# A mixture-of-experts stage on one core: slots and gather of a block three blocks ahead instead of two, and another order of units

## Chip, cores and metric

The kernel runs on one core of a Trainium2 chip. The metric is the device time of one execution in microseconds (us), the median of several runs.

## What is computed

One decoder block on 512 tokens of width 1024: a mixer (a Mamba-2 state-space branch and a short convolution), then a mixture of experts. The change touches the experts alone. Of the reference, cut:

```python
e_idx = top_k(where(expert_mask, biased, -inf), 8)[1]        # 8 of 64 experts for each token
gate = take_along_axis(scores, e_idx, axis=1); gate = gate / gate.sum(-1) * 2.5
...
xin = h_pad[row_tok].reshape(nb, 128, d)                     # tokens sorted by expert, in blocks
def expert_block(xb, e):                                     # D_EXPERT = 256
    return (silu(xb @ w_gate[e]) * (xb @ w_up[e])) @ w_down[e]
routed = segment_sum(yb * row_gate[:, None], row_tok)        # back to the tokens
x = layer_norm(ALPHA * x + g2 * (routed + shared)) * ln2_g + ln2_b
```

All is float32. The weights of the 64 experts are 3 MB each and are read once.

## The kernel before

The first 860 us (norms, projections, state-space scan, output projection, router) are not touched. The expert stage follows. Experts are ranked by their number of tokens, and each rank has a fixed number of slots (`CAPS`: 320, 192, 160, 128, 96, 64, 32). Slots are packed into **blocks** of 128: a block belongs to one expert (then matmuls run in three passes on split weights, `matmul3`, lines 153 to 155) or to two to four experts side by side in the columns of the array (`tiled`, line 950, plain fp32).

Blocks are grouped into **units** by the string `ORDER`, one word a unit, one letter a group of ranks: `x` and `y` and `z` are the large ranks with their remainders (x three blocks, y and z two), `f` a full block, `a` a 96+32 pair, `p` two times 64, `q` four times 32. So ya, za, qy, qff and faa have three blocks, ap has two; qy and qff load six experts, ya, za and ap four, faa five. The first unit (two ranks with a fixed place, one block) is ordered by the framework's scheduler; from the second on PE's order is the program's own (`manual_schedule`), while DVE, ACT, POOL and SP are ordered by the scheduler.

For each block `slots` (lines 1108 to 1135) makes, for its 128 slots, which token sits there: DVE compares positions with a counter (`oh`, line 1116), PE multiplies the one-hot with the tokens' numbers and gates (line 1124, into the one `st` bank), DVE reduces that to `red` (1127) and to the index `idx` (1129), and POOL issues an indirect DMA that gathers the 128 rows of `h2_d` into a page (line 1132; in the profile `pg<-h_d,idx`). There are `NXG` = 3 such pages, used in turn. `xsteps` (from line 897) then transposes the page in two times four PE transposes (line 150, `ps_tr<-ident,pg`, two `tr` banks), and ACT (line 911 or 158), for a block of one expert also DVE (line 160), copies the bank into `xt`.

A unit (`unit`, from line 1410) runs: gate and up matmuls of its blocks (`ps_pj`), then a mixed stretch, here called the **hand-over**: PE adds the unit before's results to the tokens (`csteps`, lines 1188 and 1189, eight steps, one part a block), with the transposes of its own activations (`ps_tr<-ident,sg`) and then those of the next unit's blocks (`xs_steps`) in between; then its down matmuls (`ps_y` of lines 153 to 155 and 950). In `xs_steps` the slots are made like this:

```python
while len(xs) < min(n, len(allb)):
    i = len(xs)
    need_s(i + 1)
    r, g = xsteps(sl[i][0], None, len(allb[i][0]) > 1)
    xs.append(r)
    yield from g
    need_s(i + NXG)
```

So after block i is transposed, blocks up to i+2 have their slots and gathers. Weights come on SP's queue (lines 869 and 872) in pieces of 1 MB, each expert's gate and up in two halves and its down, into seven pairs of pages and, for every eighth piece, one from a second pool; a piece waits until the matmuls have freed its buffer. Weights of single-expert blocks are split by ACT (line 158, `wh<-pr`) and DVE (160, `wl<-pr`).

Of the kernel before, what the change touches and what calls it, by code (L numbers as in the profile page):

```python
# [8 lines left out]
F32 = mybir.dt.float32  # L9
# [9 lines left out]
T, D, P = 512, 1024, 128  # L19
# [18 lines left out]
NXG = 3  # L38


ORDER = "x qy ya ap za qff ya ap za faa ya ap za faa p"
AHEAD = 10
NDEF = 2
FORD = "q0 r0 s0 q1 r1 s1 q2 r2 s2 q3 r3 s3"
# [19 lines left out]
def block_kernel(ctx: ExitStack, tc: tile.TileContext, a, out, dbg=None):  # L64
# [25 lines left out]
    def bank(tag, bufs, dt=F32):  # L90
        return ps.tile([P, 512], dt, name="ps_" + tag, tag=tag, bufs=bufs)
# [645 lines left out]
    rt = ctx.enter_context(tc.tile_pool(name="rt", bufs=1))  # L737
# [159 lines left out]
    def xsteps(src_ap, dst=None, whole=False):  # L897

        hi, lo = dst or [None if whole and i else hold.tile([P, KD, P], F32 if whole else FR, name="xt", tag="hm", bufs=8)
                         for i in range(2)]  # L900
        sv = src_ap.rearrange("p (d k) -> p k d", k=KD)

        def steps():
            for q in range(2):
                tp = bank("tr", 2)
                for k in range(4):
                    transpose(tp[:, k * P:(k + 1) * P], sv[:, 4 * q + k, :])
                tv = tp.rearrange("p (k n) -> p k n", k=4)
                sl_ = slice(4 * q, 4 * q + 4)
                if whole:  # L910
                    S.activation(hi[:, sl_, :], tv, AF.Copy)
                else:
                    split_to(hi[:, sl_, :], lo[:, sl_, :], tv)
                yield

        return (hi, lo), steps()
# [191 lines left out]
    def slots(*parts):  # L1108


        oh = rt.tile([P, NT, P], BF, name="oh", bufs=2)
        w = min(n for _, n, _ in parts)
        i, tiles = 0, []
        for v, n, pays in parts:
            m = len(pays)
            V.tensor_tensor(oh[:, :, i:i + n * m].rearrange("p t (q s) -> p t q s", q=m),
                            iota1[:, None, None, :n].to_broadcast([P, NT, m, n]),
                            v[:, :, :, None].to_broadcast([P, NT, m, n]), op=OP.is_equal)
            i += n * m
            tiles += [p_ for p_ in pays for _ in range(n // w)]  # L1120
        ip = bank("st", 1)
        for t in range(NT):
            for q, p_ in enumerate(tiles):
                PE.matmul(ip[w * q:w * q + w, :6], oh[:, t, w * q:w * q + w], p_[:, t],
                          start=(t == 0), stop=(t == NT - 1), tile_position=(0, w * q) if w < P else None)
        red = rt.tile([P, 2], F32, name="red", bufs=8)
        V.tensor_reduce(red, ip[:, :6].rearrange("p (a b) -> p a b", b=3), axis=AX.X, op=OP.add)
        idx = rt.tile([P, 1], I32, name="idx", bufs=4)
        V.tensor_scalar(idx, red[:, 0:1], NOTOK, None, op0=OP.add)
        xg = xgs[nblk[0] % NXG]  # L1130
        nblk[0] += 1
        GP.indirect_dma_start(out=xg, out_offset=None, in_=h2_d[:, :],  # L1132
                              in_offset=bass.IndirectOffsetOnAxis(ap=idx, axis=0),
                              bounds_check=T - 1, oob_is_err=False)
        return xg, red
# [101 lines left out]
    def static_slots(u):  # L1237
        return slots((pg[:, :, 0, u[0]:u[-1] + 1], P // len(u), [pays[:, :, e, :] for e in u]))
# [61 lines left out]
    def seg(r, n, m=1, v=None):  # L1300
        return (posp if v is None else v)[:, :, r:r + m], n, [pay[:, :, r + i, :] for i in range(m)]

    def second(r):
        pc = rt.tile([P, NT, 1], F32, name="pc")
        V.tensor_scalar(pc, posp[:, :, r:r + 1], 128.0, None, op0=OP.subtract)
        return slots((pc, P, [pay[:, :, r, :]]))
# [6 lines left out]
    for r in range(NM):  # L1313
        bl = [((0,), lambda r=r: slots(seg(r, P)))]
        if r == 0:
            bl.append(((0,), lambda r=r: second(r)))
        n = caps[r] % 128
        r2 = of[128 - n].pop(0)
        bl.append(((0, 1) if n == 64 else (0, 1, 1, 1),
                   lambda r=r, n=n, r2=r2: slots(seg(r, n, 1, posr), seg(r2, 128 - n))))  # L1320
        kinds["x" if r == 0 else "y" if n == 64 else "z"].append(((r, r2), bl))
# [5 lines left out]
    for k, n in (("p", 64), ("q", 32)):  # L1327
        m = 128 // n
        for r in of[n][::m]:
            kinds[k].append((tuple(range(r, r + m)),  # L1330
                             [(tuple(range(m)), lambda r=r, n=n, m=m: slots(seg(r, n, m)))]))
    for ks in ORDER.split():

# [18 lines left out]
    def need_s(n):  # L1352
        while len(sl) < min(n, len(allb)):
            sl.append(allb[len(sl)][1]())

    def xs_steps(n):
# [3 lines that stand above are left out]
            r, g = xsteps(sl[i][0], None, len(allb[i][0]) > 1)  # L1360
            xs.append(r)
            yield from g
            need_s(i + NXG)

    def need_x(n):
        drain(xs_steps(n))
# [43 lines left out]
    def unit(n):  # L1410


        i0, i1 = ublk[n], ublk[n] + len(units[n][1])
        i2 = i1 + len(units[n + 1][1]) if n + 1 < len(units) else i1
        need_x(i1)
        run = expert([b for b, _ in units[n][1]], units[n][2], sl[i0:i1], xs[i0:i1], lambda e, q: take((n, e, q), AHEAD))
        for _ in range(2 * len(units[n][2])):
            next(run)
        com = csteps() if parts else iter(())
        for _ in range(2):  # L1420
            next(com, None)
        for _ in range(i1 - i0):
            next(run)
            next(com, None)
        zipper(xs_steps(i2), com, islice(over_, 1))
        next(run)
        tail[0] = n + 1 == len(units)
        drain(run)
# [113 lines left out]
```

## Time and profile before

| | us |
|---|---|
| runs | 1625.51, 1630.03, 1628.57 |
| median | 1628.57 |
| the profiled execution, its own time | 1629.32 |
| its span, first to last instruction | 1627.5 |
| PE busy in the span | 1496.8 (92%) |
| mean granted clock of TensorE | 0.972 of full speed |
| expert stage, about | 860 to 1605 |

The page gives busy time by engine, then the span in 40 slices of 40.7 us each. "Granted clock" is TensorE's clock as a share of full speed. A row of the timeline has start, length, engine, line, operation, tiles written and read, shapes and count; in brackets the idle time of that engine ahead of it and what ended it. A row of waits has who waited, for whom, us in total, times, longest.

### The profile page before, as it was taken

The page shows a single profiled execution, that of the slowest core. Times are in us where ns is not written, and L with a number is a line of the kernel's source. Part 1 is how long each engine was busy: PE and PEld are TensorE (multiplying, and loading weights), DVE is VectorE, ACT ScalarE, POOL GpSimd, SP SyncE. Part 2 cuts the span into 40 slices and gives each one's busy share as a digit, 9 for nine tenths or more (in the row PEclk, how much of TensorE's full clock was granted, in tenths as well). Part 3 has the DMA queues.
Part 4 walks back from the last instruction along what each step waited for, and adds up shares of the span by engine and source line. Part 5 has one row for each costly group of instructions (what it writes and reads, how often), then busy time and mean ns, then how long its engine had stood idle before and what let it go on. Part 6 is the DMA issues. An engine that isn't in the chain of part 4 may idle for free.

```text
span 1627.5 us, 22863 instructions
## 1 busy us (share of the span) xinstructions
PE 1496.8 (92%) x8253; PEld 1018.3 (63%) x8253; DVE 974.6 (60%) x1810; ACT 645.4 (40%) x925; POOL 230.3 (14%) x232
## 2 busy tenths in 40 slices
PE   6999999999999999999978899988889988998893
PEld 3688777787777877887755544545544555554452
DVE  4558778667858556536786535545554554444456
ACT  2456575655634545334542213222341232222222
POOL 0011110111012457300135000000010000000001
PEclk9999999999999999999999999999999999999997
DMA  9653432533441667536227677877988878877671
GB/s 277 170 154 88 113 70 83 147 85 97 117 100 39 203 202 217 167 91 212 108 77 289 234 283 286 305 297 302 386 303 304 309 255 358 317 301 297 253 302 53
DMA packets 194504, 335.67 MB, mean 206 GB/s; under 512 B 13428, under 2 KB 136660, under 8 KB 186196
## 3 DMA queue, kind: packets, MB, share of 16 engines
q1 hardware_dynamic: 183300, 303.73, 53.9%
q0 software_dynamic: 11088, 30.45, 7.3%
q8 instruction: 66, 1.08, 0.3%
q14 instruction: 50, 0.41, 0.1%
HBM read 334.58 MB, written 4.28 MB: 208 GB/s over the span
## 4 chain that ended last, share of the span: by engine, by line
PE 68%; DMA 12%; DVE 8%; issue 6%; ACT 3%; POOL 1%; SPq 1%; DVEq 0%; ACTq 0%; POOLq 0%
PE ps_pj L153 12%; PE ps_pj L154 12%; PE ps_pj L155 12%; PE ps_pj L950 6%; DMA pr<-in_w_up_dram 5%; PE ps_y L950 5%; PE ps_y L1188 4%; PE ps_y L1189 4%; PE ps_tr L150 4%; DMA pg<-h_d,idx 4%; DMA pg<-in_w_ada_dram 2%; DVE wl L160 2%; PE ps_y L153 1%; PE ps_y L155 1%; PE ps_y L154 1%
## 5 line engine op out<-in xcount | busy, mean ns | idle before, releaser
L153 PE MATMUL ps_pj<-hm,wh 128*128 128x512 f32 x680 | 276.3, 407 | 2.0 <-ACT wh L158 2.0
L155 PE MATMUL ps_pj<-hm,wl 128*128 128x512 f32 x680 | 267.4, 394 | 6.2 <-DVE wl L160 6.2
L154 PE MATMUL ps_pj<-hm,wh 128*128 128x512 f32 x680 | 267.4, 393 | 0.0
L160 DVE TENSOR_TENSOR wl<-pg,wh 128x1024 fp32r<-128x1024 f32 (+1 forms) x129 | 157.1, 1224 | 116.9 <-ACT wh L158 116.7
L950 PE MATMUL ps_pj<-pr,xt 128*32 128x512 f32 (+1 forms) x1472 | 212.2, 604 | 9.7 <-DMA pr<-in_w_up_dram 9.7
L158 ACT ACTIVATE wh<-pg 128x1024 fp32r<-128x1024 f32 (+1 forms) x135 | 127.5, 952 | 136.4 <-PE ps_pj L154 104.6
L950 PEld LDWEIGHTS ps_pj<-pr,xt 128*32 128x32 f32 (+1 forms) x1472 | 62.0, 117 | 150.1 <-issue 139.7
L153 PEld LDWEIGHTS ps_pj<-hm,wh 128*128 128x128 f32 x680 | 128.9, 190 | 36.7 <-issue 6.0
L155 PEld LDWEIGHTS ps_pj<-hm,wl 128*128 128x128 f32 x680 | 128.5, 189 | 36.7 <-DVE wl L160 8.8
L154 PEld LDWEIGHTS ps_pj<-hm,wh 128*128 128x128 f32 x680 | 128.5, 189 | 28.9 <-issue 3.4
L160 DVE TENSOR_TENSOR wl<-pr,wh 128x1024 fp32r<-128x1024 f32 x72 | 86.9, 1220 | 96.6 <-ACT wh L158 96.0
L1132 POOL DMA_INDIRECT pg<-h_d,idx x41 | 48.1, 1174 | 597.2 <-PE ps_y L1189 163.6
L1194 DVE TENSOR_TENSOR res<-res,ps_y 128x512 f32<-128x512 f32 x120 | 82.2, 686 | 75.3 <-PE ps_y L1189 73.7
L150 PE MATMUL ps_tr<-ident,pg 128*128 128x128 f32 x392 | 71.1, 314 | 49.0 <-DMA pg<-h_d,idx 45.7
L158 ACT ACTIVATE wh<-pr 128x1024 fp32r<-128x1024 f32 x72 | 74.8, 1054 | 101.5 <-DMA pr<-in_w_up_dram 67.4
L950 PE MATMUL ps_y<-pr,wkr 128*32 128x512 f32 (+1 forms) x736 | 106.1, 618 | 0.8 <-DVE wk L1165 0.8
L150 PEld LDWEIGHTS ps_tr<-ident,pg 128*128 128x128 f32 x392 | 58.9, 196 | 60.5 <-issue 32.6
L1165 DVE SCALAR_TENSOR_TENSOR wk<-ps_y,red,pg 128x512 f32<-128x512 f32 x82 | 61.0, 748 | 35.3 <-PE ps_y L155 20.1
L366 POOL TENSOR_TENSOR pg<-pg 128x1024 f32<-128x1024 f32 x28 | 74.1, 2665 | 54.6 <-ACT pg L364 54.5
L927 ACT ACTIVATE sg<-ps_pj 128x256 f32<-128x256 f32 x44 | 16.8, 384 | 159.7 <-PE ps_pj L950 99.2
L153 PE MATMUL ps_pj<-pg,wh 128*128 128x512 f32 x192 | 76.0, 396 | 1.3 <-ACT zs L431 1.2
L155 PE MATMUL ps_pj<-pg,wl 128*128 128x512 f32 x192 | 76.3, 397 | 0.0
(394 smaller groups left out, 2648.8 us busy)
## 6 DMA issues: line engine op xcount, KB each, us to landing
pr<-in_w_gate_dram SPq DMA_DIRECT2D x128, 512.0 KB, 9.8
pr<-in_w_up_dram SPq DMA_DIRECT2D x128, 512.0 KB, 10.1
pr<-in_w_down_dram SPq DMA_DIRECT2D x64, 1024.0 KB, 11.7
pg<-in_w_in_dram SPq DMA_DIRECT2D x88, 512.0 KB, 4.9
pg<-in_w_ada_dram SPq DMA_DIRECT2D x48, 512.0 KB, 5.9
bc<-acs_d POOLq DMA_DIRECT2D x32, 256.0 KB, 4.5
pg<-in_w_ssd_out_dram SPq DMA_DIRECT2D x16, 512.0 KB, 4.5
pg<-in_w_sc_out_dram SPq DMA_DIRECT2D x8, 512.0 KB, 4.0
```

The costliest lines, as they stand in the source:

```text
L150: return PE.transpose(o, i, ident[:n, :n])
L153: PE.matmul(o, lh, rh, start=start, stop=False)
L154: PE.matmul(o, lh, rl, start=False, stop=False)
L155: PE.matmul(o, ll, rh, start=False, stop=stop)
L158: S.activation(hi, src, AF.Copy)
L160: V.tensor_tensor(lo, src, rw(hi), op=OP.subtract)
L366: GP.tensor_tensor(part[i], part[i], w, op=OP.add)
L950: PE.matmul(o[w * i:w * i + w, :], x[:, w * i:w * i + w], m, start=start, stop=stop, tile_position=(0, w * i))
L1165: V.scalar_tensor_tensor(yg, o, red[:, 1:2], g2b[:, ns_], op0=OP.mult, op1=OP.mult)
L1188: PE.matmul(o, oh_, yh[:, ns_], start=(i == 0), stop=False)
L1189: PE.matmul(o, oh_, yl[:, ns_], start=False, stop=(i == len(ps_) - 1))
L1194: V.tensor_tensor(ra[t][:, ns_], ra[t][:, ns_], o, op=OP.add)
```

## The change

After block i is transposed, slots and gather are made up to block i+3. `red` has ten buffers in place of eight. The same units come in another order: qy third instead of second among the words of `ORDER`, faa twice behind ap instead of behind za.

```diff
-ORDER = "x qy ya ap za qff ya ap za faa ya ap za faa p"
+ORDER = "x ya qy za ap ya qff za ya ap faa za ap faa p"
@@ slots
-        red = rt.tile([P, 2], F32, name="red", bufs=8)
+        red = rt.tile([P, 2], F32, name="red", bufs=10)
@@ xs_steps
-            need_s(i + NXG)
+            need_s(i + 1 + NXG)
```

First place: PE, the hand-over at the end of unit x, in which the next unit's blocks are transposed (`ps_tr<-ident,pg`; x4 is half a block) between steps of the combine (`ps_y<-pr,oht`). Before, from the end of the next unit's first block on; rows of line 1124 are slots (`pay` the tokens' numbers and gates), and of each run of them the first two are shown:

```order
L150 MATMUL ps_tr<-ident,pg 128x128 x4
L1188 MATMUL ps_y<-pr,oht 128x512
L1189 MATMUL ps_y<-pr,oht 128x512
L1124 LDWEIGHTS oh
L1124 MATMUL ps_st<-pay,oh 64x6
...
L150 MATMUL ps_tr<-ident,pg 128x128 x4
L1188 MATMUL ps_y<-pr,oht 128x512
L1189 MATMUL ps_y<-pr,oht 128x512
L150 MATMUL ps_tr<-ident,pg 128x128 x4
L1124 LDWEIGHTS oh
L1124 MATMUL ps_st<-pay,oh 128x6
...
L150 MATMUL ps_tr<-ident,pg 128x128 x8
```

Now, the same stretch:

```order
L150 MATMUL ps_tr<-ident,pg 128x128 x4
L1188 MATMUL ps_y<-pr,oht 128x512
L1189 MATMUL ps_y<-pr,oht 128x512
L1124 LDWEIGHTS oh
L1124 MATMUL ps_st<-pay,oh 32x6
...
L150 MATMUL ps_tr<-ident,pg 128x128 x4
L1188 MATMUL ps_y<-pr,oht 128x512
L1189 MATMUL ps_y<-pr,oht 128x512
L150 MATMUL ps_tr<-ident,pg 128x128 x4
L1124 LDWEIGHTS oh
L1124 MATMUL ps_st<-pay,oh 128x6
...
L150 MATMUL ps_tr<-ident,pg 128x128 x8
```

The pattern is the same; the slots in it are other blocks'. Before, the 64x6 rows make the slots of the very block (qy's third) that the x8 row transposes. Now the 32x6 rows make those of the first block of the unit after (qy's q), and the slots of the block in the x8 row (ya's third) stood ahead of unit x's down and gate matmuls.

Second place: ACT at the hand-over of an ap unit, behind its two `silu` rows (`sg`). `xt` rows empty banks of transposed blocks, `wh<-pr` rows split weights of the coming unit's single-expert block. Before, at all three ap units, and now at the first and third:

```order
L941 ACTIVATE wkr<-ps_tr 128x256 x2
L158 ACTIVATE xt<-ps_tr 128x512 x2
L911 ACTIVATE xt<-ps_tr 128x512
L158 ACTIVATE wh_76<-pr 128x1024
L911 ACTIVATE xt<-ps_tr 128x512
L158 ACTIVATE wh_78<-pr 128x1024
L911 ACTIVATE xt<-ps_tr 128x512 x2
```

Now, at the second ap unit:

```order
L941 ACTIVATE wkr<-ps_tr 128x256 x2
L158 ACTIVATE xt<-ps_tr 128x512 x2
L911 ACTIVATE xt<-ps_tr 128x512 x2
L158 ACTIVATE wh_76<-pr 128x1024
L158 ACTIVATE wh_78<-pr 128x1024
L911 ACTIVATE xt<-ps_tr 128x512 x2
```

There the two splits stand together, ahead of the last block's copies.

Third place: DVE in the first unit. The first `red` and `idx` on either side are those of unit x's third block (the `posr` row belongs to a block of ya); `wl_77` is the lower half of a split weight. One piece of the difference:

```order
-L1160 TENSOR_SCALAR tok<-red 128x1
-L1161 TENSOR_SCALAR oht<-iota_t,tok 128x512
-L160 TENSOR_TENSOR wl_77<-pr,wh_76 128x1024
-L1127 TENSOR_REDUCE red<-ps_st 128x2
-L928 TENSOR_TENSOR sg<-sg,ps_pj 128x256
-L1129 TENSOR_SCALAR idx<-red 128x1
...
+L1127 TENSOR_REDUCE red<-ps_st 128x2
+L1116 TENSOR_TENSOR oh<-iota_5824,posr 128x4x64
+L1129 TENSOR_SCALAR idx<-red 128x1
...
+L160 TENSOR_TENSOR wl_77<-pr,wh_76 128x1024
```

The index is now made ahead of the weight split, not behind it. On PE the slots' matmuls of that block stand nine matmuls (`ps_pj<-pr,xt 64x512`) earlier: before they follow a run of eleven of these, now a run of two. And of unit x's second and third block the transposes now stand, half a block at a time, between the first unit's down matmuls (`ps_y<-pr,wkr 64x512`).

## Rows read from the trace of the kernel before

**Rows 1.** The page, the span in 40 slices: busy tenths of PE and of the DMA engines.

```profile
PE   6999999999999999999978899988889988998893
...
DMA  9653432533441667536227677877988878877671
```

**Rows 2.** PE's waits from 930 to 1600 us: who waited for whom, us in total, times, longest.

```profile
PE ps_tr L150 <- DMA pg<-h_d,idx: 41.8, 10, 5.4
PE ps_pj L950 <- DMA pr<-in_w_up_dram: 9.7, 8, 1.6
PE ps_pj L154 <- DVE wl L160: 4.8, 6, 1.0
```

**Rows 3.** The timeline of all engines in the hand-over from za to qff, 1122 to 1129 us.

```profile
1122.14 0.25 PE L1124 MATMUL ps_st<-pay,oh 128*128 128x6 bf16 x4
...
1123.01 0.40 PE L1189 MATMUL ps_y<-pg,oht 128*128 128x512 f32 x1
...
1123.25 0.40 PE L1188 MATMUL ps_y<-hm,oht 128*128 128x512 f32 x1
1123.35 0.14 DVE L1129 TENSOR_SCALAR idx<-red 128x1 int32<-128x1 f32 x1
...
1123.72 0.61 PE L150 MATMUL ps_tr<-ident,pg 128*128 128x128 f32 x4
...
1124.23 0.99 POOL L1132 DMA_INDIRECT pg<-h_d,idx  x1 [34.86 <-PE ps_y L1189]
1124.36 0.60 ACT L158 ACTIVATE xt<-ps_tr 128x512 fp32r<-128x512 f32 x1 [0.78 <-PE ps_tr L150]
1124.99 0.69 DVE L160 TENSOR_TENSOR xt<-ps_tr,xt 128x512 fp32r<-128x512 f32 x1
...
1128.56 1.94 PE L150 MATMUL ps_tr<-ident,pg 128*128 128x128 f32 x8 [4.16 <-DMA pg<-h_d,idx]
```

**Rows 4.** The chain of work that ended last, in unit x's start: start, us, what.

```profile
888.36 11.16 DMA pg<-h_d,idx
```

**Rows 5.** Seven us from the end of each of the ten waits for a gathered page on: stretch, length, PE busy (matmuls), granted clock, DMA share, GB/s.

```profile
933.80:940.80 7.00, 7.00 (x35) 0.76 0.43 130
991.80:998.80 7.00, 6.96 (x50) 0.76 0.43 126
1084.70:1091.70 7.00, 6.95 (x50) 0.79 0.21 60
1128.60:1135.60 7.00, 7.00 (x44) 0.76 0.23 75
1186.00:1193.00 7.00, 6.96 (x50) 0.76 0.28 74
1279.90:1286.90 7.00, 6.99 (x68) 1.00 0.34 108
1323.90:1330.90 7.00, 6.96 (x31) 0.56 0.30 92
1378.90:1385.90 7.00, 6.96 (x32) 0.59 0.32 96
1471.60:1478.60 7.00, 6.95 (x56) 0.63 0.36 104
1517.90:1524.90 7.00, 7.00 (x36) 0.77 0.03 10
```

**Rows 6.** The same columns for gaps in the weights' stream, from the last landing of one period to SP's next issue, nine of them at hand-overs with such a wait: three of the nine, and the sum of all nine.

```profile
1278.60:1284.60 6.00, 4.68 (x56) 1.00 0.30 99
...
1378.40:1389.20 10.80, 10.26 (x60) 0.71 0.21 63
1471.00:1478.70 7.70, 7.05 (x56) 0.63 0.33 96
...
sum 81.50, PE 69.16; mean PE 7.68
```

**Rows 7.** The same columns for a stream of weights between two gaps, faa behind za.

```profile
1334.50:1378.20 43.70, 38.89 (x290) 1.00 0.97 370
```

**Rows 8.** The timeline of PE at the first unit's start, where two halves of a block are transposed close together.

```profile
876.62 0.71 PE L150 MATMUL ps_tr<-ident,pg 128*128 128x128 f32 x4 [0.69 <-ACT xt L911]
```

**Rows 9.** PE's waits in unit qy's gate and up matmuls (945 to 970 us, the first row) and in qff's (1137 to 1170 us).

```profile
PE ps_pj L950 <- DMA pr<-in_w_up_dram: 3.0, 2, 1.6
...
PE ps_pj L950 <- DMA pr<-in_w_up_dram: 3.2, 2, 1.6
PE ps_pj L154 <- DVE wl L160: 1.5, 2, 0.8
PE ps_pj L153 <- ACT wh L158: 0.5, 1, 0.5
```

**Rows 10.** The timeline of PE in the first unit and at unit x's third block.

```profile
883.51 2.74 PE L950 MATMUL ps_pj<-pr,xt 128*64 128x512 f32 x11
...
899.65 0.95 PE L150 MATMUL ps_tr<-ident,pg 128*128 128x128 f32 x4 [1.90 <-DMA pg<-h_d,idx]
```

**Rows 11.** ACT's waits for weight pieces from 930 to 1600 us, and a split of weights in ACT's timeline at the hand-over of an ap unit.

```profile
ACT wh L158 <- DMA pr<-in_w_up_dram: 64.5, 12, 9.5
...
1077.49 1.05 ACT L158 ACTIVATE wh<-pr 128x1024 fp32r<-128x1024 f32 x1
```

**Rows 12.** The columns of rows 5 for a hand-over whose next unit has two blocks, without a wait.

```profile
1425.00:1432.00 7.00, 7.00 (x50) 1.00 0.40 116
```

## The prediction

> **What bounds the kernel now.** I read the page's slices first, then TensorE's waits in the expert stage, then one hand-over between two units row by row, then the granted clock and the DMA share in short windows. From slice 22 on (the expert stage, about 930 to 1600 us) PE is 80 to 90% and more busy, and the DMA engines 60 to 90% [rows 1]: neither is full, so something stops both. PE's waits name it: 41.8 us in ten waits of the transposes for a gathered page, against 9.7 us for weights and 4.8 us for a split weight [rows 2].
>
> The hand-over shows why [rows 3]. The 1122.14 row makes the slots of the coming unit's third block, after that unit's first block was transposed; its index is ready at 1123.35, POOL issues the gather at 1124.23. PE has one more block to transpose (until about 1124.4), then it stands for 4.16 us, until the page has landed and the 1128.56 row starts. The third block's gather is issued some 4 us before it is needed, with nothing left to cover its landing. Units with two blocks have no such wait: both gathers are a unit old.
>
> The wait has a second price. [...] At a hand-over without a wait the clock stays at 1.00 [rows 12].
>
> **The change, part by part.** (a) *Three ahead.* After block i is transposed, the slots of i+3 instead of i+2 are made. Its page is the one that block i has just left (three pages), so no new wait on POOL for a page arises; PE, POOL and SP issue the same instructions as before, with other blocks' slots at the old places. All blocks of a unit, third one too, now have their gathers issued during the hand-over before: one unit earlier, 44 us between the third and fourth wait [rows 5]. The longest flight in the trace, under full weight traffic, is 11.16 us [rows 4]. So the ten waits go: **-41.8 us** [rows 2].
>
> (b) *The clock they cost.* Per window, lost time is (1 - granted share) x 7 us: 0.24+0.24+0.21+0.24+0.24+0+0.44+0.41+0.37+0.23 = 2.62, times 7 = **-18.3 us** [rows 5]. None of it stays if no other pause follows.
>
> (c) *What is late next on PE.* Two blocks are now transposed back to back at each three-block hand-over, through two banks. The last four transposes need the bank of the four before the previous ones, which ACT empties in 0.60 us, with 0.69 us on DVE behind it for a block of one expert [rows 3]. The nearest row of a transpose waiting for that is 0.69 us [rows 8]. Bounds per hand-over: 0 (the slots' matmuls and four transposes cover it) and 0.60 + 0.69 = 1.3. I take 0.69, since it is that very wait: **+6.9 us** over ten (0 to 13).
>
> (d) *Weights.* SP can load about eight 1 MB pieces ahead (seven pairs and one page pair); it waits for a unit's down matmuls to free them. Order, not work, changes: the same fifteen units. Between the first release of one unit and that of the next it loads the old unit's downs and twice the new unit's experts, less what was preloaded; so qy brings 2+12 = 14 MB now and 4+12 = 16 MB behind ya, as qff does today. PE's weight waits are 3.0 us in qy today and 3.2+1.5+0.5 = 5.2 us in qff [rows 9]: I take the difference, **+2.2 us**. Both faa now follow ap instead of za, so their period is shorter by one part's combine, 16 matmuls 0.24 us apart [rows 3], 3.8 us, for the same 14 MB; today the DMA needs 43.7 us for that [rows 7] and then has a gap of 10.8 [rows 6]. I price this at nothing, covered by that gap; if the cover is gone it costs up to 3.8 us twice. Bounds for (d): 0 and 2.2 + 7.6 = 9.8.
>
> Is the gap large enough for (a) and (b)? SP's releases come after the wait and after the slow stretch, so from one release to the next hand-over nothing moves; what shrinks is the DMA's gap before the next release. The nine gaps at the later waits are 6.0 to 12.4 us long, 81.5 us in all, at shares of 0.11 to 0.46 [rows 6]; the tightest, 1471.0 to 1478.7, is 7.7 us and loses about 4.2 (the mean wait) + 2.6 (its slow stretch) = 6.8. It fits, barely.
>
> (e) *Start.* The third block of unit x waits 1.90 us for a gather that started at 888.36 [rows 4, 10]. The new order makes its slots nine of the x11 matmuls of the 883.51 row earlier, 9/11 of 2.74 = 2.2 us [rows 10], more than the wait: **-1.9 us** (0 to -3.6 with a slow stretch behind it; above zero, +3, if the transposes now placed between the first unit's down matmuls hold those up). (f) `red` from 8 to 10 buffers: nine blocks' results can be alive; no instruction, nothing on the path.
>
> Sum against the profiled execution (1629.3 us; the median of the runs is 1628.6, so within 0.1%): 1629.3 - 41.8 - 18.3 - 1.9 + 6.9 + 2.2 = **1576.4 us**.
>
> **The rivals.** *R1, weights take part of it back.* If the DMA's gaps cannot go under the shortest one seen, 6.0 us, the nine give 81.5 - 9 x 6.0 = 27.5 us, and the first wait, whose gap is wide, 4.2 + 1.7 = 5.9; (c) then hides in the weights' wait. 1629.3 - 33.4 - 1.9 + 2.2 = **1596 us**. For it: a stream between two gaps takes 0.97 of the DMA engines [rows 7], and the gaps hold the next gathers too. Against it: in a gap the share is 0.11 to 0.46 and SP is the one that waits [rows 6].
>
> *R2, the clock is not given back.* The hand-over becomes a run of transposes and short matmuls; if the clock fell there without a wait, (b) would be lost: 1576.4 + 18.3 = **1595 us**. Against it: hand-overs without a wait, transposes included, show 1.00 [rows 12], and the sixth window shows 1.00 although a wait and a block's transposes stand there [rows 5]. [...]
>
> *R3, slower: ACT blocked by a weight copy.* ACT works in order, and at hand-overs copies of coming weights stand between the copies that empty the transposes' banks (the second place shown with the change). Today such a copy at 1077.49 starts without a wait, while ACT's waits for weights, 12 with up to 9.5 us, fall into the gate and up matmuls [rows 11]. If weights fell behind so far that this copy waited 9.5 us at each of ten hand-overs, PE would stand behind it: 1576.4 + 95 = **1671 us**. It turns slower than before once the copy is over 5.3 us late on each (53 / 10). Against it: that needs the DMA stream to be late at every hand-over, and only two or three of the periods have no slack.
>
> *R4, it doesn't do what it says.* If the gather were still issued at the old time (held on POOL behind the page or an index), nothing would change: **1629 us**. Against it: at the new place the page is free and the slots' matmuls stand in PE's order a whole unit before the transposes that need them.
>
> **How the numbers follow.** Forecast with its own bounds 0.65; R1 0.20; R2 0.07; R3 0.05; R4 0.03. The predicted time is 1576 us. Low end 1560: (c) and (d) at zero give 1567.3, (e) at its best 1565.6, and some of today's weight waits (9.7 us) may end with the denser run. High end 1603: the forecast with (c), (d) and (e) at their worst is 1576.4 + 6.1 + 7.6 + 4.9 = 1595, and it takes in R1 and R2 with half of (c) on top. R3 and R4 lie outside, with a few hundredths of the rest. About 0.3% (4.9 us) is what a measurement of this kernel can tell from no change. Faster by more: 0.65 + 0.20 + 0.07 = 0.92; within: 0.03; slower: 0.05.
>
> **What would show it.** Right: PE's waits for the gathered page in the expert stage fall from ten to none, or under 3 us; the granted clock after hand-overs is 1.00; small new waits of the transposes for ACT's or DVE's copies, under 1 us each; the DMA's gaps shrink from 6 to 12 us to 1 to 6; qy waits about 5 us for weights. R1 would show as PE waits for weight pieces of 2 to 4 us in most units; R2 as slow stretches without a pause ahead; R3 as transposes waiting for ACT while ACT waits for a weight; R4 as unchanged gather waits. The forecast is wrong if the ten waits go and the time falls by less than 30 us.

## The result, and the profile after

| | before | changed |
|---|---|---|
| median, us | 1629.30 (1625.51 to 1632.53, 4 runs) | 1583.97 (1580.36 to 1588.03, 4 runs) |
| profiled execution, us | 1629.32 | 1580.36 |
| its span, us | 1627.5 | 1578.6 |
| mean granted clock | 0.972 | 0.983 |

The changed kernel takes 0.972 of the time, with a 95% interval of 0.969 to 0.976: 45 us less. The forecast was 1576 us, in a range of 1560 to 1603. The profiled execution is the fastest of the four.

The page's slices of the changed kernel, PE, the granted clock and the DMA engines, answer to [rows 1]:

```profile
PE   6999989999999999999988999999988999999994
PEclk9999999999999999999999999999999999999997
DMA  9763423632531557634622967998989788997871
```

From slice 23 on PE now shows 8 or 9 tenths in every slice but the last, and the DMA engines 6 to 9. PE's waits from 930 to 1555 us answer to [rows 2] (who waited for whom, us in total, times, longest); eight of the ten largest are:

```profile
PE ps_pj L950 <- DMA pr<-in_w_up_dram: 11.7, 10, 2.3
PE ps_pj L154 <- DVE wl L160: 6.0, 7, 1.7
PE ps_pj L153 <- ACT wh L158: 3.2, 3, 1.4
PE ps_y L154 <- DVE wl L160: 1.6, 1, 1.6
...
PE ps_st L1124 <- DVE oh L1116: 0.8, 1, 0.8
PE ps_tr L150 <- ACT xt L911: 0.8, 1, 0.8
PE ps_tr L150 <- DVE xt L160: 0.6, 1, 0.6
PE ps_st L1124 <- DVE red L1127: 0.4, 1, 0.4
```

The gathered page is no longer among them: 41.8 us in ten waits have become none. The waits for weights and their splits (first four rows) have grown from 14.5 us, and 0.9 for splits by ACT, to 22.5. The hand-over from za to ya in the changed kernel, rows of the timeline of all engines, stands against [rows 3]:

```profile
1253.83 0.60 PE L150 MATMUL ps_tr<-ident,pg 128*128 128x128 f32 x4
...
1254.36 0.29 PE L1124 MATMUL ps_st<-pay,oh 128*64 128x6 bf16 x8
...
1254.59 1.25 PE L150 MATMUL ps_tr<-ident,pg 128*128 128x128 f32 x8
...
...
1256.99 1.12 POOL L1132 DMA_INDIRECT pg<-h_d,idx  x1 [46.96 <-DVE idx L1129]
```

The third block's eight transposes start at once behind the second block's. The gather that POOL issues at 1256.99 is for a block of the unit after ya and has a whole unit to land (the stage's gathers took 3.9 to 9.6 us from issue to landing). The 7 us behind each of the ten three-block hand-overs (columns as in [rows 5]):

```profile
924.20:931.20 7.00, 7.00 (x39) 1.00 0.51 156
970.40:977.40 7.00, 7.00 (x49) 1.00 0.54 168
1022.60:1029.60 7.00, 6.68 (x46) 1.00 0.61 199
1110.10:1117.10 7.00, 6.65 (x50) 1.00 0.45 144
1150.60:1157.60 7.00, 6.17 (x36) 0.76 0.56 187
1206.50:1213.50 7.00, 5.39 (x55) 1.00 0.73 231
1255.80:1262.80 7.00, 6.73 (x53) 1.00 0.40 116
1342.60:1349.60 7.00, 7.00 (x65) 1.00 0.52 166
1386.20:1393.20 7.00, 6.73 (x53) 1.00 0.81 317
1474.60:1481.60 7.00, 7.00 (x48) 1.00 0.30 96
```

Nine of ten are at 1.00, where nine of ten were at 0.56 to 0.79. The tenth stands behind two new pauses, in the hand-over before qff: a transpose waits 0.58 us for DVE's `xt` at 1149.89, the slots 0.83 us for `oh` at 1151.54.

For a sum I take one stretch whose ends are the same work in every kernel: from the end of the wait for `wkr` that opens the expert stage to the end of the last combine's wait for `rww`. First before, then the changed kernel (columns as above):

```profile
862.12:1599.12 737.00, 670.05 (x4204) 0.97 0.79 297
```

```profile
858.64:1549.98 691.34, 658.60 (x4205) 0.99 0.84 316
```

The stage is 45.7 us shorter: PE idles 34.2 us less (67.0 to 32.7) and is busy 11.4 us less. The span fell by 48.9; the remaining 3.2 us lie outside the stage, nearly all ahead of it, where nothing was changed.

### The profile page after: what moved, and what is told of

It reads as the page before. It is cut to its first block, busy times and chain, and to the rows that moved or that the text cites. A ratio compares the mean times of both kernels' runs of the same rounds, so it can differ in the third digit from the quotient of the medians.

```text
span 1578.6 us, 22869 instructions
## 1 busy us (share of the span) xinstructions
PE 1486.1 (94%) x8253; PEld 1010.2 (64%) x8253; DVE 975.3 (62%) x1810; ACT 644.8 (41%) x925; POOL 227.3 (14%) x232
## 4 chain that ended last, share of the span: by engine, by line
PE 73%; DMA 11%; DVE 8%; ACT 3%; issue 2%; POOL 1%; SPq 1%; DVEq 0%; ACTq 0%; POOLq 0%
PE ps_pj L153 12%; PE ps_pj L154 12%; PE ps_pj L155 12%; PE ps_pj L950 8%; DMA pr<-in_w_up_dram 8%; PE ps_y L950 5%; PE ps_y L1188 5%; PE ps_y L1189 5%; PE ps_tr L150 4%; DMA pg<-in_w_ada_dram 2%; DVE wl L160 2%; PE ps_y L153 1%; PE ps_y L155 1%; PE ps_y L154 1%; PE ps_y L483 1%
## 5 line engine op out<-in xcount | busy, mean ns | idle before, releaser
L950 PE MATMUL ps_y<-pr,wkr 128*32 128x512 f32 (+1 forms) x736 | 102.7, 596 | 1.3 <-DVE wk L1165 1.3
L928 DVE TENSOR_TENSOR sg<-sg,ps_pj 128x256 f32<-128x256 f32 x44 | 18.3, 420 | 111.8 <-ACT sg L927 111.8
L153 PE MATMUL ps_pj<-pg,wh 128*128 128x512 f32 x192 | 75.9, 395 | 1.1 <-ACT zs L431 1.1
L154 PE MATMUL ps_pj<-pg,wh 128*128 128x512 f32 x192 | 75.8, 395 | 0.0
L416 DVE SCALAR_TENSOR_TENSOR wk<-ps_pj,cw,wk 128x511 f32<-128x511 f32 (+2 forms) x93 | 68.3, 742 | 7.4 <-ACT wk L414 7.0
```

The lines of the kernel that those rows point to most:

```text
L153: PE.matmul(o, lh, rh, start=start, stop=False)
L154: PE.matmul(o, lh, rl, start=False, stop=False)
L416: V.scalar_tensor_tensor(acc[:, s:], o[:, :T - s], cw[:, 3 - s, tl:tl + 1], acc[:, s:], op0=OP.mult, op1=OP.add)
L950: PE.matmul(o[w * i:w * i + w, :], x[:, w * i:w * i + w], m, start=start, stop=stop, tile_position=(0, w * i))
```

## The experiments

The question that the result left: the prediction's sum, without its term for weights and order, gives 1574 us, and the kernel came out 10 us above. So the two halves of the change were run apart, the price of the clock by itself, and then the order's parts and the weights. Times stand beside runs of the kernel before on the same chip. The stage columns are worked out as above, from each profiled execution; the last column is PE's busy time while the granted clock was at its lower level, 0.50 of full speed (in before's trace from 1129 to 1132 us, in the changed kernel's from 1455.2 to 1458.5, for example).

| run | median, us | ratio to before | stage | PE busy | idle | busy at lower clock |
|---|---|---|---|---|---|---|
| before, profiled as above | 1629.3 | 1 | 737.0 | 670.1 | 67.0 | 46.8 |
| e0 change again | 1584.4 | 0.970 (0.967 to 0.974) | 690.1 | 658.4 | 31.7 | 9.8 |
| e1 three ahead, old order | 1574.0 | 0.965 (0.962 to 0.968) | 677.5 | 651.8 | 25.7 | 0 |
| e2 two ahead, new order | 1639.8 | 1.003 (1.000 to 1.006) | 748.9 | 681.4 | 67.5 | 69.9 |
| e3 the wait filled | 1617.5 | 0.990 (0.986 to 0.994) | 723.4 | 692.8 | 30.6 | 15.6 |
| e4 qy second, faa behind ap | 1580.8 | 0.969 (0.966 to 0.972) | 690.9 | 659.2 | 31.8 | 17.1 |
| e5 qy third, faa behind za | 1576.5 | 0.967 (0.964 to 0.970) | 684.1 | 655.9 | 28.2 | 6.8 |
| e6 change, half of the downs | 1579.5 | 0.967 (0.964 to 0.971) | 686.0 | 659.7 | 26.3 | 13.1 |
| e7 old order, half of the downs | 1577.1 | 0.966 (0.963 to 0.969) | 684.8 | 657.3 | 27.5 | 12.7 |
| e8 change, half of gate and up | 1558.7 | 0.955 (0.952 to 0.958) | 667.9 | 647.1 | 20.8 | 14.4 |
| e9 old order, half of gate and up | 1552.0 | 0.952 (0.949 to 0.955) | 657.2 | 640.6 | 16.7 | 3.4 |

Before's median was 1634.2 us beside e0 to e3, 1631.5 beside e4 to e7 and 1629.9 beside e8 and e9. The stage columns are of one execution each, and not always a typical one: e1's is the second fastest of its eight (1566.4 us) and e9's the fastest, while those of e0, e4, e6 and e8 are the slowest or second slowest of theirs. So stage differences between these are larger than those of the medians.

**The two halves apart: e0, e1, e2.** e0 is the changed kernel again. e1 is the changed kernel with the order of before; e2 is the kernel before with the new order:

```diff
e1, against the change
-ORDER = "x ya qy za ap ya qff za ya ap faa za ap faa p"
+ORDER = "x qy ya ap za qff ya ap za faa ya ap za faa p"
e2, against before: the same line the other way round
```

> The changed kernel once more, so that the three beside it are compared with it under the same conditions. Theory (the gathered page of a third block comes a unit earlier, ten waits and the slow clock behind them go): 1584 us, ratio to before 0.972.

> Three blocks ahead with the old order of units, so the first part alone. Theory (the lead of the gather is the whole gain, the order adds only weight waits): no PE wait for a gathered page left, ratio 0.969 to 0.972, 1579 to 1584 us; the waits for f's split weight in the two faa units, 2.2 + 2.2 us and 1.3 us for a weight in the changed kernel, are back at about 1.2 us each, and qy waits about 3 us for weights in place of 5. Rival (the order is needed for the gain, since units with much to load come in the wrong place once the pauses are gone): over 1595 us, with PE waits for weight pieces above 25 us in all.

> The new order with slots and gather two blocks ahead as before, so the second part alone. Theory (the order alone removes no gather wait, and moves at most some weight waits): ten PE waits for a gathered page, about 42 us, and 1628 to 1635 us, ratio 0.999 to 1.004. Rival (the order has a part in the gain): under 1620 us.

All of the gain comes from three blocks ahead. e1 came out 5 us under the low end of what was expected of it, so the order costs more than was thought then. e1 ran at 1560.8 to 1577.8 us (8 runs), e0 at 1580.1 to 1591.5 (6 runs): the ranges don't touch, and the new order costs 10 us beside it. With two ahead the order gains nothing (e2, 5.6 us above before in the medians, at the edge of what can be told); its ten waits for gathered pages are still there, 39.1 us. e1's stage:

```profile
857.88:1535.35 677.47, 651.77 (x4204) 1.00 0.85 323
```

Against before's 737.0 and 670.05, with the same order: idle time is 41.3 us less and busy time 18.3 us less, and none of the busy time is at the lower clock. That holds for this execution: it and one other have the highest granted clock of e1's eight runs, 0.988; the others have 0.980 to 0.986. The clock is not all that sets e0 and e1 apart: among the runs with 0.980 or 0.981, e0's three took 1580.1 to 1589.8 us and e1's three 1574.3 to 1577.8.

**The price of the clock alone: e3.** The kernel before, with four matmuls on constants ahead of each third block's transposes (`third` holds those blocks), into a bank that is free there:

```diff
+            if i in third:
+                fill = bank("pj", 3)
+                for k in range(NFILL):                        # NFILL = 4
+                    PE.matmul(fill, ident, iota_t, start=(k == 0), stop=(k == NFILL - 1))
```

> The kernel before, with four idle fp32 matmuls of 128x512 (about 3.5 us together, their result is not used) put on PE ahead of the transposes of each third block, where PE waits for the gathered page. The gathers come as late as before, so this shows the price of the clock alone. Theory (each of the ten waits costs 1.5 to 3 us more through the slow clock behind it): the granted clock behind the hand-overs is 1.00, and the time is 1612 to 1618 us, ratio 0.990 to 0.994. Rival (the clock costs little, since what runs behind the wait is not bound by the array's clock): 1625 to 1631 us.

The waits in e3's stage (columns as above), and the fill's own group of instructions (its number and form, then busy us and mean ns):

```profile
PE ps_pj L951 <- DMA pr<-in_w_up_dram: 9.7, 8, 2.2
PE ps_tr L151 <- DMA pg<-h_d,idx: 6.8, 7, 1.9
```

```profile
L1367 PE MATMUL ps_pj<-iota_t,ident 128*128 128x512 f32 x80 | 36.9, 604 | 0.0
```

The 80 records are the 40 matmuls, two each. The third block is no earlier: fill and what is left of the wait make 36.9 + 6.8 = 43.7 us, where the wait alone was 41.8. PE merely works through it, and the kernel is 16.7 us faster in the medians. Without the fill's 36.9 us PE is busy 655.9 us in the stage, 14.1 less than before. So the clock behind a pause is a cost of its own, and near the size that (b) gave it; 15.6 us of e3's work is still at the lower level.

**Which part of the order: e4 and e5.** Both are three ahead. e4 puts qy back to second place and leaves the rest of the new order, e5 moves qy alone:

```diff
e4
+ORDER = "x qy ya za ap ya qff za ya ap faa za ap faa p"
e5
+ORDER = "x ya qy ap za qff ya ap za faa ya ap za faa p"
```

> Three blocks ahead, with qy second as before and the rest of the order as in the change (faa behind ap, qff between ya and za). The full order of the change gave 1584.4 us, the order of before 1574.0. Theory: the price of the order, about 10 us, lies behind qff and in faa behind ap (a shorter period for the same weights), not in qy: 1584 us here, with waits of 1.3 to 1.5 us for up weights in both faa. Rival: qy third is what costs; then this kernel stands at about 1574.

> Three blocks ahead, the order of before with qy moved to third place alone (faa behind za). Theory (faa behind ap and the neighbours of qff cost, qy does not): 1574 us, waits in faa of 0.8 us and no slow clock behind them. Rival (qy third costs): 1584 us, with the waits for weights in qy and ap at 980 to 1050 us larger than the 4 us of the change.

By the ratio e4 stands 0.001 under e0, e5 0.002 above e1, and the intervals of all four overlap their neighbours'. The order of the four is as the theory has it. In the stage e4 has 690.9 us with 31.8 idle, as e0 has, but e5 has 684.1 with 28.2, about halfway between e1 and e0. The rival's sign is there too: e5's waits for weights and a split between 980 and 1060 us are 5.4 us, where the changed kernel's between 980 and 1050 are 3.6. So faa behind ap and qff between ya and za may carry most of the price, but this is not shown: by time e4 and e5 are not told apart.

**Less of the weights: e6 and e7.** Half of each down piece:

```diff
-            SY.dma_start(r, wd.rearrange("(p k) n -> p k n", k=2))
+            SY.dma_start(r[:, 0], wd.rearrange("(p k) n -> p k n", k=2)[:, 0, :])
...
-            return ... else held[e][:, q - 4, :]
+            return ... else held[e][:, 0, :]
```

> The change, but only half of each down piece is loaded (0.5 MB instead of 1 MB; its first half is used twice), so 2.5 MB an expert instead of 3. PE's, ACT's and DVE's work and the order stay. Theory: what is left between the order of the change and that of before is late weights and the slow clock behind them; with a sixth less to load PE's waits for weights (22 us in the change) fall under 8 us, and the time to about 1560 us, within 3 us of the same cut with the order of before. Rival (the order costs on PE, ACT and DVE themselves, by copies that stand in another order at the hand-overs): the waits fall, but this kernel stays some 10 us above the next one.

> Three blocks ahead, the order of before, half of each down piece loaded as in the run before this one. Theory: 1574.0 less about 10 us of its 15 us of waits for weights, so 1562 us, within 3 us of the run before this one. Rival: some 10 us below that run.

The two kernels are 2.4 us apart, as expected, but at 1579 and 1577 us, not near 1560: there the expectation failed. PE's waits for weights and splits, 22.3 us in e0, came to 16.9, not under 8, and those for up pieces did not fall at all (12.7 in e0), with a sixth less to load:

```profile
PE ps_pj L950 <- DMA pr<-in_w_up_dram: 12.7, 10, 1.6
PE ps_pj L154 <- DVE wl L160: 4.0, 5, 1.1
```

So these waits don't follow the bytes of a period. In e6, ahead of faa behind ap, SP waited 16.1 us for free pages, and PE then waited for pieces issued after that (a row of waits, then the first piece behind the release and PE's first wait for one):

```profile
SPq L869 <- PE ps_y L950: 16.1, 1, 16.1
```

```profile
1352.02 0.34 SPq L869 DMA_DIRECT2D pr<-in_w_gate_dram  x1
...
1367.48 3.64 PE L950 MATMUL ps_pj<-pr,xt 128*32 128x512 f32 x32 [1.12 <-DMA pr<-in_w_up_dram]
```

A page comes free only when the unit's down matmuls have used it, and from there on it is a burst: twelve half-megabyte gate and up pieces, and PE's first wait for one of them begins 14.3 us after the release.

**The burst itself: e8 and e9.** Half of each gate and up piece instead, the downs whole:

```diff
-                SY.dma_start(r[:, i], w.rearrange("(p k) n -> p k n", k=KD)[:, 4 * q:4 * q + 4, :])
+                SY.dma_start(r[:, i, :2], w.rearrange("(p k) n -> p k n", k=KD)[:, 4 * q:4 * q + 2, :])
...
-            return held[e][:, :, q % 2 * 2:q % 2 * 2 + 2, :] if q < 4 else ...
+            return held[e][:, :, :2, :] if q < 4 else ...
```

> The change, but only half of each gate and up piece is loaded (0.5 MB instead of 1 MB, the loaded half used twice), the downs whole. The engines' work, the order and the number of pages stay. Halving the downs left the waits for up weights at 12.7 us, since in faa behind ap SP stood idle for 16 us until the ap unit's down matmuls freed the pages, and PE then waited for gate and up pieces issued behind that release. Theory now: the waits are that burst between release and need. With half of it PE's waits for up weights and for the splits (22 us in the change) fall under 5 us, no slow clock stays behind them, and the kernel comes to 1565 us, within 3 us of the same cut with the order of before. Rival (the order's price lies on the engines themselves): the waits fall as well, but this kernel stays 8 us or more above the next one.

> Three blocks ahead, the order of before, half of each gate and up piece loaded as in the run before this one. Theory: waits for up weights and splits from 15 us to under 5, time about 1563 us, within 3 us of the run before this one. Rival: 8 us or more below that run.

e8's waits for up pieces:

```profile
PE ps_pj L950 <- DMA pr<-in_w_up_dram: 0.6, 1, 0.6
```

The burst is confirmed: 12.7 us of waits (e0) become 0.6, and in e9 none. Both kernels are faster than expected (1565 and 1563 us); the last section bears on that. What I had made of the burst is not confirmed: e8 stays 6.7 us above e9. That is under the rival's 8 and over the theory's 3, and the intervals overlap at their ends. By this pair some 4 of the order's 10 us are late weights; by e6 and e7, where 2.4 us are left with the waits for up pieces still there, it would be nearly all, so the share is not settled. In the two profiles e8 has 4.1 us more idle and 6.5 us more busy, and in the busy part 14.4 us at the lower clock against 3.4. Two pauses of e8 that stand ahead of such a stretch (PE's timeline) are in the hand-over before qff, as in the changed kernel:

```profile
1153.82 0.71 PE L150 MATMUL ps_tr<-ident,pg 128*128 128x128 f32 x4 [0.58 <-DVE xt L160]
...
1155.43 0.25 PE L1124 MATMUL ps_st<-pay,oh 128*32 128x6 bf16 x13 [0.78 <-DVE oh L1116]
```

In e9 no wait for `oh` is over 0.3 us. But most of e8's low clock need not belong to the order: some 8 of its 14.4 us stand in the stage's first 40 us, and so do all of e9's 3.4; of the changed kernel's two profiles one has a stretch there (e0, at 897.5) and the other none.

**What stays open.** How the order's 10 us split between waits for weights and splits (7.4 us more in the changed kernel's profile than in e1's), waits for DVE, the clock behind them and chance is not settled: the pieces are small, and runs of one kernel spread by 6 to 21 us.

## Why the prediction was right, and where its size was off

The direction, the mechanism and the range held; the point was 8 us low. By its own steps:

**(a) Ten waits go, -41.8 us: right.** Ten waits to none, so R4 falls. Its sentence that "no new wait on POOL for a page arises" is in doubt: by the profile four of POOL's waits from 915 us on now end with a transpose (74.9 us in all, none before). POOL is idle there anyway (55.3 us busy in the stage's 691.3), and PE waits for none of these gathers.

**(b) The clock behind them, -18.3 us: near in size, with luck in it, and its condition failed.** With the order of before PE's busy time fell by 18.28 us in the stage (e1), and e3 shows the price apart. That the number is met so closely is luck: (b) priced the 36.6 us of work at the lower clock behind the ten waits at half their length (1 - 0.50), while e1 got back 18.28 us for 46.8 us, three more stretches included (899.9, 968.2 and 1258.3), which is 0.39 for each, and e3 14.1 for 31.2, which is 0.45. The condition was "None of it stays if no other pause follows". In the changed kernel other pauses follow: 13.1 us of PE's work is still at the lower clock, at 1151.4, 1185.5, 1455.2 and 1503.0, each behind a wait for weights, a split or DVE, and the busy time fell by 11.4 only. Nor does every such pause bring the clock down: before, two waits of 1.56 and 1.42 us (965.64, 968.08) end in such a stretch; in e1 two of 1.54 and 1.42 us (952.35, 954.79, shown in the last section) leave the clock at 1.00. R2 falls, since the hand-overs without such pauses ran at 1.00 (nine of the ten windows above). Eight transposes between matmuls were followed by a lower clock at one hand-over of ten (0.76 in the window from 1150.60 on), and that one had pauses of 0.58 and 0.83 us; a stretch of transposes alone was not tried.

**(c) Back-to-back blocks, +6.9 us: over-sized.** Visible waits of the transposes for ACT's and DVE's copies are 0.8 + 0.6 us, and of the slots for DVE 0.8 + 0.4: 2.6 us at ten hand-overs. In seven of them the copies had kept up, as the 1254.59 row shows.

**(d) Weights and order, +2.2 us: the step that was mis-sized.** Order and all cost 10.4 us in the medians (e0 against e1). The sum without (d) is 1574.2 us, and e1 measured 1574.0, or 0.965 of before, which is 1572 beside a before of 1629.3; as (c) was too dear and (b) counted on no slow clock, part of that agreement is luck. The 2.2 us did not come where they were put: PE's waits for weights in unit qy are 2.1 us and 0.5 for a split, not about 5. Longer waits came at both faa behind ap instead. The sentence that failed there is "I price this at nothing, covered by that gap". The waits at faa behind ap are these rows of PE in the changed kernel:

```profile
1365.41 3.59 PE L950 MATMUL ps_pj<-pr,xt 128*32 128x512 f32 x26 [1.31 <-DMA pr<-in_w_up_dram]
1370.42 0.50 PE L153 MATMUL ps_pj<-wh,xt 128*128 128x512 f32 x1 [1.42 <-ACT wh L158]
1371.68 0.50 PE L154 MATMUL ps_pj<-wl,xt 128*128 128x512 f32 x1 [0.76 <-DVE wl L160]
```

3.5 us, and 2.5 at the second faa (1496.24 to 1502.51), against 0.95 us for the same three matmuls behind za in e1, and 0.8 at its second faa:

```profile
1308.69 3.59 PE L950 MATMUL ps_pj<-pr,xt 128*32 128x512 f32 x26 [0.18 <-DMA pr<-in_w_up_dram]
1312.29 0.50 PE L153 MATMUL ps_pj<-wh,xt 128*128 128x512 f32 x1
1313.55 0.50 PE L154 MATMUL ps_pj<-wl,xt 128*128 128x512 f32 x1 [0.77 <-DVE wl L160]
```

A gap did lie ahead of the changed kernel's faa: between these two rows of SP's queue it issued nothing, and the DMA share fell to 0.24 (windows of 2 us):

```profile
1333.77 0.34 SPq L869 DMA_DIRECT2D pr<-in_w_up_dram  x1
1346.34 0.34 SPq L869 DMA_DIRECT2D pr<-in_w_gate_dram  x1
```

```profile
1344.34:1346.34 2.00, 2.00 (x22) 1.00 0.24 37
```

But the gap ends with the release, and the waited-for pieces come after it; a period's bytes against a period's length don't tell when these land. There is one more difference in the rows. The last two gathers of this hand-over start 2.3 and 0.6 us before the release, and fly with its first pieces:

```profile
1344.08 1.33 POOL L1132 DMA_INDIRECT pg<-h_d,idx  x1 [3.58 <-DVE red L1127]
1345.71 1.68 POOL L1132 DMA_INDIRECT pg<-h_d,idx  x1 [0.30 <-issue]
```

In e1, ahead of its release at 1290.38, they start at 1283.88 and 1286.20, and the third half-megabyte piece lands 6.4 us after its issue, not 8.1. That the gathers cause this was not tried alone. These waits and the slow clock behind one of them (1503.0) are part of (d)'s excess; how much of the rest is weights at all stays open (e6 to e9). R1 named the effect (weights take part back) but priced it through the DMA's gaps, by the same error.

**(e) The start, -1.9 us: right, and a little more.** The 1.90 us wait is gone, and so is one of 2.0 us for a gather at 893.24. The transposes between the first unit's down matmuls hold nothing up (PE's timeline):

```profile
886.45 1.07 PE L950 MATMUL ps_y<-pr,wkr 128*64 128x512 f32 x2
887.46 0.71 PE L150 MATMUL ps_tr<-ident,pg 128*128 128x128 f32 x4
888.09 1.08 PE L950 MATMUL ps_y<-pr,wkr 128*64 128x512 f32 x4
```

**R3** (ACT blocked by a weight copy) did not occur: transposes wait for ACT once, 0.8 us.

In the stage's account: idle was to fall by 41.8 + 1.9 - 6.9 - 2.2 = 34.6 us and fell by 34.2, two errors that cancel ((c) too dear, (d) too cheap). What is missing to the forecast is the busy time, 11.4 for 18.3.

## What to carry to other kernels

When PE waits for a transfer in a fixed place of the program, ask first how long ahead its issue stands; one block more of look-ahead, with buffers already there, was worth 3.5% here, and about a third of that was the clock behind the pause (18.3 us less busy time in e1's stage), which can be measured alone by filling the pause with idle matmuls (14.1 us in e3). A transfer that is limited by free buffers is judged from the release to the need, not by bytes over a period: here a gap of the DMA engines ahead of the release (share 0.24 in its last 2 us) did not keep PE from waiting 3.5 us behind it. Run the halves of a change apart: the faster kernel here is e1, look-ahead without the new order, at 0.965 (0.962 to 0.968) of before.

## What the runs showed that was not expected

In these runs PE's busy time itself changed with the weights that were loaded. The gate and up matmuls, before the bar the busy time and the mean of one, then the idle time in front, in e0 and in e8, whose weights are half loaded:

```profile
L950 PE MATMUL ps_pj<-pr,xt 128*32 128x512 f32 (+1 forms) x1472 | 214.3, 600 | 12.7 <-DMA pr<-in_w_up_dram 12.7
```

```profile
L950 PE MATMUL ps_pj<-pr,xt 128*32 128x512 f32 (+1 forms) x1472 | 200.5, 594 | 0.6 <-DMA pr<-in_w_up_dram 0.6
```

The same 1472 matmuls, each about as long, take 13.8 us less busy time in all, on top of the idle time saved; e1 against e9 gives 211.8 and 199.4. With half of the downs instead it did not fall (215.5 in e6). The rows of one block of four experts, side by side in the columns of the array, show what fills that time. In e1, with whole pieces, then the same block of the same unit in e9, with half pieces:

```profile
948.96 1.85 PE L950 MATMUL ps_pj<-pr,xt 128*32 128x512 f32 x4
952.35 1.02 PE L950 MATMUL ps_pj<-pr,xt 128*32 128x512 f32 x2 [1.54 <-DMA pr<-in_w_up_dram]
954.79 3.62 PE L950 MATMUL ps_pj<-pr,xt 128*32 128x512 f32 x26 [1.42 <-DMA pr<-in_w_up_dram]
```

```profile
958.92 3.64 PE L950 MATMUL ps_pj<-pr,xt 128*32 128x512 f32 x32
```

In e9, where the four experts' matmuls start together, the 32 records take 3.64 us. In e1 PE started those whose pieces had landed, six records one behind the other in 1.85 + 1.02 us, and the rest in 3.62: 2.85 us more busy time, besides 2.96 us of idle. So this block's late pieces cost PE's busy time too. Over the stage, of the 288 groups of four such records, all start together (each within 60 ns of the one before) in e9 and 278 in e8, 258 in e1 and in e0, and 250 in e6. That this makes up the whole 13.8 us was not worked out.
